# The norms of a fused ten-phase block go to the head of every engine's row, and one MLP leaves another tile of each half to its end

## The chip, the cores and the metric

The kernel runs on one core of a Trainium2 chip. The metric is the device time of one execution in microseconds; the median of several runs is compared. A core has a matrix engine (TensorE, PE in the rows; PEld is its weight load), VectorE (DVE), ScalarE (ACT), GpSimd (POOL) and SyncE (SP, which issues most transfers here). Each of these engines takes its instructions from its own row, one after the other; semaphores make it wait for the others.

## The reference

Two residual blocks run one after the other on x of 256 x 1024 in float32. The first has four sublayers (windowed attention, squared-ReLU MLP, a gated recurrent block, MLP), each modulated by a condition c, the second has six (feed-forward, hybrid mixer, feed-forward, twice). Cut to what matters here:

```
def layer_norm(x, g, b):
    mu = mean(x); var = mean((x - mu)**2)
    return (x - mu) * rsqrt(var + 1e-5) * g + b

for i in range(2):                              # first block
    shift, scale, gate = split(silu(c) @ ada_w[i, 0] + ada_b[i, 0])
    y = mixer(x * (1 + scale) + shift)          # attention (i = 0) or recurrent block (i = 1)
    x = layer_norm(sqrt(2) * x + (1 + gate) * y, ln_g[i, 0], ln_b[i, 0])
    shift, scale, gate = split(silu(c) @ ada_w[i, 1] + ada_b[i, 1])
    y = square(relu((x * (1 + scale) + shift) @ w1[i])) @ w2[i]
    x = layer_norm(sqrt(2) * x + (1 + gate) * y, ln_g[i, 1], ln_b[i, 1])
# the second block has the same norm behind each of its six sublayers, without shift, scale and gate
```

So there are ten norms. Four of them stand behind a modulated sublayer, and the first three also stand in front of one.

## The kernel before

x stays on the chip as two tiles of 128 rows (X[0] and X[1], in the rows X_76 and X_77: the two "halves"). The ten phases run one after the other, in the order attn, mlp0, rnn, mlp1, ffn00, mix0, ffn01, ffn10, mix1, ffn11. Weights stream in from HBM in units of 128 x 2048 (raw, L346). ScalarE rounds each tile of a unit to a part hi (L365; VectorE by a copy at L363 for some), and VectorE subtracts this to get lo (L369). Activations are split likewise (L382 on ScalarE, L384 on VectorE, into tT and hT). Each product is then three matmuls, hi x hi, hi x lo and lo x hi: L393 to L395 and L402 to L404 for the first matrix of a phase (into pu), L429 to L431 for the second one (into four accumulators acc[half, c], c being a half of the 1024 columns).

A phase's second matrix comes in tiles (class Down): 32 in an MLP, 22 in a feed-forward, 8 in the attention, 12 in the recurrent block. The last LAG = 4 tiles of each half are left for the end (`tail`), so that half 0 can be finished while TensorE still has half 1 to do. `finish` (L691) then goes, for each half, through the tail's matmuls, the norm (`ln_stats`, L628) and the turn to the layout of the next phase (`turn`, L653).

The norm's steps for one half, each on 512 columns where nothing else is said: t = acc x g1 (L636, only behind a modulated sublayer), X = sqrt(2) X + t (L638), statistics (L639), then aggregation (L641) and adding epsilon (L642) on one column, the power -1/2 on GpSimd (L643). In front of a modulated phase L650 makes the bias and ScalarE normalises (L652). In the other norms (`ln["direct"]`) VectorE does it in two steps (L646, L648). Then TensorE transposes eight blocks of 128 x 128 (L661), and these are evacuated with shift and scale by VectorE and ScalarE in turn (L668, L670) or by ScalarE alone (L663) into h. TensorE multiplies this h by the first, unsplit weights of the next phase in plain float32 (head_mm, L688; each of these instructions has two records in the profile).

Other work runs alongside the norms on VectorE: the first weight splits of the next phase, in quarters of 256 columns for the first seven tiles (L369), and the sums of the next modulations (aacc, L481 and L483, one step per row of 128 of the ada matrix).

What sets the order: the program is written in one sequence, and a scheduler merges it into one row per engine, by rank of each instruction (its place in the program, with instructions under `tc.high_priority()` ahead of all others) and by its own estimate of when operands are ready. `turn` is under `tc.high_priority()` already. At the six norms ahead of an unmodulated phase TensorE's row is written by hand (`tc.manual_schedule`): tail of half 0, tail of half 1 without its last product, turn of half 0, the last product, matmuls of the next phase, turn of half 1.

Of the kernel before, what the change touches and what calls it, by code (L numbers as in the profile page):

```python
# [25 lines left out]
LAG = 4  # L26
# [24 lines left out]
ADA = {"attn": (0, 0), "mlp0": (0, 1), "rnn": (1, 0), "mlp1": (1, 1)}  # L51
# [3 lines left out]
def nf(ph):  # L55

    return NF.get(ph, 3)
# [47 lines left out]
def items_of(ph):  # L105

    if ph == "attn":
        out = [("k", 0), ("k", 1), ("v", 0), ("v", 1)] + [("q", h) for h in range(4)]
        for h in range(8):
            if h < 4:  # L110
                out.append(("q", h + 4))
            if h >= 2:
                out.append(("o", h - 2))
        return out + [("o", 6), ("o", 7)]
    if ph in ("mlp0", "mlp1"):
        return ff_items(32, ("u",))
    if ph.startswith("ffn"):
        return ff_items(22, ("g", "u"))
    if ph == "rnn":
        x = [("x", t) for t in range(12)]  # L120
        g = [("g", t) for t in range(12)]
        b = [("b", j) for j in range(12)]
        o = [("o", k) for k in range(12)]
        return (x[:5] + b[:3] + g[:1] + x[5:8] + b[3:6] + g[1:3] + x[8:] + b[6:9] + g[3:6] + b[9:] + o[:3] + g[6:9] + o[3:6]
                + g[9:] + o[6:])
    out = [("ka", 0), ("ka", 1), ("k", 0), ("va", 0), ("va", 1), ("va", 2), ("qa", 0)]
    name = {"c": lambda n: MIX_CONVS[n + 1], "q": lambda n: ("qa", n), "g": lambda n: ("ga", n)}
    out += [name[ev](n) for ev, n in mix_seq() if ev in name]
    for j in range(8):
        out += [("ba", j)] if ("ga", j) in out else [("ga", j), ("ba", j)]  # L130
        if j % 4 == 3:
            out += [("z", j // 4, q) for q in range(4)]
    out += [("gb", j) for j in range(4)]
    for j in range(8):
        out.append(("bb", j))
        if j < 4:
            out.append(("gb", j + 4))
        if j >= 2:
            out.append(("o", j - 2))
    return out + [("o", 6), ("o", 7), ("pad", 0)]  # L140
# [147 lines left out]
def fused_kernel(ctx, tc, x, wst, adaw, ada0, rows, rowc, cols, vecs, relb, cst, m1, rope, oh, out, phases=PH_ALL):  # L288
# [14 lines left out]
    def ps_acc(name="pa"):  # L303
        return pacc.tile([128, 512], F32, tag="acc", name=name)
# [101 lines left out]
    def joined(pool, ps, tag):  # L406

        if ps.shape[1] == 256:
            return ps
        t = pool.tile([128, 256], F32, tag=tag, bufs=3, name=tag)  # L410
        S.activation(out=t, in_=ps[:, 256:512], func=AF.Copy)
        V.tensor_tensor(out=t, in0=ps[:, 0:256], in1=t, op=ALU.add)
        return t
# [138 lines left out]
    def ada_tasks(lst, pe=False):  # L552
        seq = [(i, s, p, k) for i, s, p in lst for k in range(8)]
        for n in range(len(seq) + 5):
            def task(n=n):
                if n < len(seq):
                    ada_load(*seq[n])
                if pe:
                    if 0 <= n - 3 < len(seq) and (n - 3) % 2:
                        ada_mm(*seq[n - 4])  # L560
                    if n >= 5 and seq[n - 5][3] == 7:
                        ada_end(*seq[n - 5][:3])
                    return
                if 0 <= n - 3 < len(seq):
                    ada_mac(*seq[n - 3])
                if n >= 5 and seq[n - 5][3] == 7:
                    ada_sum(*seq[n - 5][:3])
            side.append(task)
# [57 lines left out]
            ln["ha"], ln["hb"] = ha, hb  # L626

    def ln_stats(half, acc, last):  # L628
        pool = ln["pool"]
        stt = pool.tile([128, 2, 6], F32, tag="st", bufs=2, name="stt")  # L630
        cs_ = [slice(c * 512, c * 512 + 512) for c in range(2)]
        src = [acc[half, c] for c in range(2)]
        for c, s in enumerate(cs_):
            if ln["g1"] is not None:
                t = pool.tile([128, 512], F32, tag="t1", bufs=2, name="t1")
                V.tensor_tensor(out=t, in0=src[c], in1=ln["g1"][:, s], op=ALU.mult)  # L636
                src[c] = t
            V.scalar_tensor_tensor(out=X[half][:, s], in0=X[half][:, s], scalar=SQ2, in1=src[c], op0=ALU.mult, op1=ALU.add)  # L638
            V.bn_stats(out=stt[:, c, :], in_=X[half][:, s])  # L639
        mv = pool.tile([128, 3], F32, tag="mv", bufs=2, name="mv")  # L640
        V.bn_aggr(out=mv[:, 0:2], in_=stt)  # L641
        V.tensor_scalar(out=mv[:, 1:2], in0=mv[:, 1:2], scalar1=LN_EPS, scalar2=None, op0=ALU.add)  # L642
        G.tensor_tensor(out=mv[:, 2:3], in0=mv[:, 1:2], in1=mhalf[:, 0:1], op=ALU.pow)  # L643
        if last:
            for s in cs_:
                V.scalar_tensor_tensor(out=X[half][:, s], in0=X[half][:, s], scalar=mv[:, 0:1], in1=ln["g"][:, s], op0=ALU.subtract, op1=ALU.mult)  # L646
            for s in cs_:
                ins = V.scalar_tensor_tensor(out=X[half][:, s], in0=X[half][:, s], scalar=mv[:, 2:3], in1=ln["b"][:, s], op0=ALU.mult, op1=ALU.add)  # L648
            return ins
        V.scalar_tensor_tensor(out=mv[:, 1:2], in0=mv[:, 0:1], scalar=-1.0, in1=mv[:, 2:3], op0=ALU.mult, op1=ALU.mult)  # L650
        for s in cs_:
            S.activation(out=X[half][:, s], in_=X[half][:, s], func=AF.Identity, scale=mv[:, 2:3], bias=mv[:, 1:2])  # L652
# [89 lines left out]
    class Down:  # L742


        def __init__(self, n):
            self.n, self.k, self.acc, self.tail = n, 0, {}, {0: [], 1: []}

        def add(self, t, w):
            if not self.acc:
                self.acc = {(h, c): ps_acc("acc") for h in range(2) for c in range(2)}  # L750
            if self.k >= self.n - LAG:
                for half in range(2):
                    self.tail[half].append((t, w))
            else:
                for half in range(2):
                    self.part(half, t, w, self.k == 0)
            self.k += 1
# [114 lines left out]
    def ph_mlp(ph, nxt):  # L872
        pool = state["es"].enter_context(tc.tile_pool(name="ml", bufs=1))
        tT = {}
        dn = Down(32)
        if ph == "mlp0":
            ada_tasks([(0, 1, 2)] + ([(1, 0, p) for p in range(3)] + [(1, 1, 0)] if nxt in ADA else []))
        else:
            ada_tasks([(1, 1, 2)])
            if has_mix:  # L880
                side.insert(0, lambda: bias_load(pool))
                side.append(bias_table)
        for it in items_of(ph):
            if it[0] == "u":
                u = joined(pool, up(ph, *it), "u")
                r = pool.tile([128, 256], F32, tag="r", bufs=3, name="r")
                if it[1] < nf(ph):
                    S.activation(out=r, in_=u, func=AF.Relu)
                    V.tensor_tensor(out=r, in0=r, in1=u, op=ALU.mult)
                else:  # L890
                    V.scalar_tensor_tensor(out=r, in0=u, scalar=0.0, in1=u, op0=ALU.max, op1=ALU.mult)
                t = tT[it[1]] = pool.tile([128, 512], F32R, tag="tT", bufs=LAG + 5, name="tT")
                split(t[:, 0:256], t[:, 256:512], r)
            else:
                if it[1] == 14:
                    xs_todo = x_scale()
                if it[1] in (18, 19) and xs_todo:
                    xs_todo.pop(0)()
                if it[1] == 27:
                    while side:  # L900
                        side.pop(0)()
                    ln_open(ph, nxt)
                w = get(ph, *it)
                dn.add(tT.pop(it[1]), w)
        return dn
# [183 lines left out]
    def bias_load(pool):  # L1089
        rb = pool.tile([32, 16], F32, name="rb")  # L1090
        nc.gpsimd.dma_start(out=rb, in_=relb)
        ohs = pool.tile([32, 128], F32, name="ohs")
        nc.gpsimd.dma_start(out=ohs, in_=oh)
        ext = pool.tile([16, 384], F32, name="ext")
        G.memset(ext, -1e30)
        state["bias"] = rb, ohs, ext
# [650 lines left out]
    for n, ph in enumerate(phases):  # L1747
        nxt = phases[n + 1] if n + 1 < len(phases) else None
# [9 lines left out]
        dn = f(ph, nxt)  # L1758
# [20 lines left out]
```

## Time and profile before

| | us |
|---|---|
| median of 3 runs (lowest to highest) | 2088.3 (2087.17 to 2094.09) |
| the profiled execution | 2087.69 |
| its span, first to last instruction | 2086.0 |
| TensorE busy in it | 2027.6 |
| VectorE busy | 1516.6 |
| ScalarE busy | 1116.8 |

The span is what the profile's lines cover; the profiled execution's own time has 1.7 us more around it. A timeline's row gives the start, the busy time, the engine, the line, the operation, what it writes from what it reads, the shape and the count, and in brackets the idle time of the engine just before, with the instruction that ended it. Consecutive equal instructions share a row.

### The profile page before, as it was taken

What the parts mean: (1) busy time and instruction counts of PE and PEld (TensorE: products, weight loads), DVE (VectorE), ACT (ScalarE), POOL (GpSimd) and SP (SyncE); (2) the same over time, 40 slices, a digit from 0 to 9 for tenths busy, and PEclk for the clock granted to TensorE, in tenths of its full rate; (3) what the DMA queues carried; (4) which work ended last, traced back from release to release, by engine and by line L of the source; (5) the groups of instructions that cost most, each with busy time, mean ns of one, the idle gap of its engine ahead of it and who ended that gap; (6) DMA issues with size and microseconds to landing.
All of it is one profiled execution on the core that took longest, in us unless ns stands there. A gap on an engine that the chain in (4) does not pass through costs nothing. (4 is left out here: it accounts for less than half of the span.)

```text
span 2086.0 us, 34685 instructions
## 1 busy us (share of the span) xinstructions
PE 2027.6 (97%) x13786; PEld 1777.3 (85%) x13786; DVE 1516.6 (73%) x2735; ACT 1116.8 (54%) x1995; POOL 122.3 (6%) x157
## 2 busy tenths in 40 slices
PE   6999999989999999999999999999999999999998
PEld 4788888978888888888989888888889888998886
DVE  2689989987667666789956766676668897667665
ACT  3554446874544555477644455545546774445553
POOL 0000000000000000021011000000001111100000
PEclk9999999999999999999989999999999998999999
DMA  8978884355673655454424465555546434355552
GB/s 335 336 265 329 319 319 183 129 198 187 217 254 131 241 190 194 172 182 140 157 81 180 161 224 195 187 195 189 188 156 215 136 141 157 123 201 182 194 190 81
DMA packets 67698, 409.67 MB, mean 196 GB/s; under 512 B 8240, under 2 KB 8544, under 8 KB 27088
## 3 DMA queue, kind: packets, MB, share of 16 engines
q1 hardware_dynamic: 59952, 383.25, 50.5%
q0 software_dynamic: 7440, 24.03, 3.6%
q8 instruction: 108, 1.77, 0.3%
q14 instruction: 54, 0.44, 0.1%
q10 hardware_dynamic: 144, 0.18, 0.0%
HBM read 406.34 MB, written 4.24 MB: 197 GB/s over the span
## 5 line engine op out<-in xcount | busy, mean ns | idle before, releaser
L369 DVE TENSOR_TENSOR lo<-raw,hi 128x1024 fp32r<-128x1024 f32 (+2 forms) x689 | 729.1, 1069 | 308.8 <-ACT hi L365 299.1
L365 ACT ACTIVATE hi<-raw 128x1024 fp32r<-128x1024 f32 x578 | 605.3, 1053 | 338.2 <-PE pu L402 73.9
L402 PE MATMUL pu<-hT,hi 128*128 128x512 f32 x1760 | 439.2, 392 | 0.0
L402 PEld LDWEIGHTS pu<-hT,hi 128*128 128x128 f32 x1760 | 324.6, 188 | 65.2 <-issue 0.4
L429 PE MATMUL acc<-hi,tT 128*128 128x512 f32 x688 | 271.6, 396 | 3.2 <-ACT tT L382 3.0
L430 PE MATMUL acc<-hi,tT 128*128 128x512 f32 x688 | 271.6, 395 | 0.0
L393 PE MATMUL pu<-hT,hi 128*128 128x256 f32 x928 | 271.4, 292 | 0.0
L431 PE MATMUL acc<-lo,tT 128*128 128x512 f32 x688 | 270.2, 393 | 0.0
L395 PE MATMUL pu<-hT,lo 128*128 128x256 f32 x928 | 265.5, 286 | 2.3 <-DVE lo L369 2.3
L394 PE MATMUL pu<-hT,hi 128*128 128x256 f32 x928 | 265.5, 286 | 0.0
L404 PEld LDWEIGHTS pu<-hT,lo 128*128 128x128 f32 x1760 | 240.2, 191 | 17.1
L404 PE MATMUL pu<-hT,lo 128*128 128x256 f32 x1760 | 245.6, 283 | 0.0
L393 PEld LDWEIGHTS pu<-hT,hi 128*128 128x128 f32 x928 | 178.9, 193 | 12.9 <-issue 10.6
L382 ACT ACTIVATE tT<-r 128x256 fp32r<-128x256 f32 x152 | 63.1, 416 | 235.6 <-DVE r L918 136.9
L394 PEld LDWEIGHTS pu<-hT,hi 128*128 128x128 f32 x928 | 179.1, 193 | 3.0 <-issue 2.6
L395 PEld LDWEIGHTS pu<-hT,lo 128*128 128x128 f32 x928 | 178.9, 193 | 2.7 <-DVE lo L369 2.5
L429 PEld LDWEIGHTS acc<-hi,tT 128*128 128x128 f32 x688 | 130.0, 189 | 29.6 <-ACT tT L382 5.0
L431 PEld LDWEIGHTS acc<-lo,tT 128*128 128x128 f32 x688 | 129.8, 189 | 27.7 <-issue 0.4
L430 PEld LDWEIGHTS acc<-hi,tT 128*128 128x128 f32 x688 | 130.1, 189 | 24.4 <-DVE tT L384 1.6
L688 PE MATMUL hd<-h,raw 128*128 128x128 f32 x960 | 111.4, 276 | 0.0
L688 PEld LDWEIGHTS hd<-h,raw 128*128 128x128 f32 x960 | 109.5, 192 | 1.1
L384 DVE TENSOR_TENSOR tT<-r,tT 128x256 fp32r<-128x256 f32 x152 | 64.6, 426 | 54.8 <-ACT tT L382 54.8
(398 smaller groups left out, 2755.2 us busy)
## 6 DMA issues: line engine op xcount, KB each, us to landing
raw<-wst SPq DMA_DIRECT2D x316, 1024.0 KB, 4.8
aw<-adaw SPq DMA_DIRECT2D x80, 512.0 KB, 6.5
aw<-ada SPq DMA_DIRECT2D x16, 512.0 KB, 7.6
bias<-bias_d POOLq DMA_DIRECT2D x32, 192.0 KB, 2.8
g<-rows POOLq DMA_DIRECT2D x10, 512.0 KB, 4.7
b<-rows POOLq DMA_DIRECT2D x10, 512.0 KB, 5.7
bias_d<-ext_d POOLq DMA_DIRECT2D x1, 2048.0 KB, 20.2
gbc<-g_d POOLq DMA_DIRECT2D x4, 512.0 KB, 4.4
```

Source lines behind the costliest of these rows:

```text
L365: S.activation(out=hi[:, 0:n], in_=r, func=AF.Copy)
L369: V.tensor_tensor(out=lo[:, c:c + m], in0=r[:, c:c + m], in1=hi[:, c:c + m].bitcast(F32), op=ALU.subtract)
L384: (eng or V).tensor_tensor(out=dlo, in0=src, in1=dhi.bitcast(F32), op=ALU.subtract)
L393: T.matmul(ps, lhsT=hi[:, c], rhs=r[:, 0:256], start=kk == 0, stop=False)
L394: T.matmul(ps, lhsT=hi[:, c], rhs=r[:, 256:512], start=False, stop=False)
L395: T.matmul(ps, lhsT=lo[:, c], rhs=r[:, 0:256], start=False, stop=kk == KT - 1)
L402: T.matmul(ps, lhsT=hi[:, kk * 128:kk * 128 + 128], rhs=rhs(kk), start=kk == 0, stop=False)
L404: T.matmul(ps[:, 0:256], lhsT=lo[:, kk * 128:kk * 128 + 128], rhs=rhs(kk)[:, 0:256], start=False, stop=kk == KT - 1)
L429: T.matmul(ps, lhsT=th, rhs=hi, start=first, stop=False)
L430: T.matmul(ps, lhsT=tl, rhs=hi, start=False, stop=False)
L431: T.matmul(ps, lhsT=th, rhs=lo, start=False, stop=last)
L688: T.matmul(ps[:, half * 128:half * 128 + 128], lhsT=w[:, kk * 128:kk * 128 + 128], rhs=state["h32", half][:, kk, :], start=kk == 0, stop=k ...
```

## The change

Two edits. `ln_stats` now calls the old body, renamed `ln_steps`, under `tc.high_priority()`: this holds for all ten norms and for both halves. And `Down` takes the number of tiles to leave for the end; `ph_mlp` gives it five instead of four where the next phase is a modulated one. Of the two MLPs only mlp0 (followed by rnn) is that; mlp1 is followed by ffn00 and keeps four. The buffers stay as they are.

```diff
     def ln_stats(half, acc, last):
+        with tc.high_priority():
+            return ln_steps(half, acc, last)
+
+    def ln_steps(half, acc, last):
+
         pool = ln["pool"]
...
-        def __init__(self, n):
-            self.n, self.k, self.acc, self.tail = n, 0, {}, {0: [], 1: []}
+        def __init__(self, n, tail=LAG):
+            self.n, self.k, self.acc, self.tail, self.last = n, 0, {}, {0: [], 1: []}, tail
...
-            if self.k >= self.n - LAG:
+            if self.k >= self.n - self.last:
...
-        dn = Down(32)
+
+        dn = Down(32, LAG + 1 if nxt in ADA else LAG)
```

The new kernel's lines are five (norm, turn) or six (further down) higher: L636 is L641 there, L638 is L643, L639 is L644, L641 is L646, L642 is L647, L646 is L651, L648 is L653, L650 is L655, L661 is L666, L668 is L673, L688 is L693.

VectorE at the first norm (attention to mlp0), before; the names t_ are the products with g1, the first two of half 76 and then two of half 77:

```order
L639 BN_STATS stt<-X_76 128x6 x2
L636 TENSOR_TENSOR t_1209<-acc,g_1117 128x512
L641 BN_AGGR mv<-stt 128x2
L636 TENSOR_TENSOR t_1213<-acc,g_1117 128x512
L642 TENSOR_SCALAR mv<-mv 128x1
L638 SCALAR_TENSOR_TENSOR X_77<-X_77,t_1209 128x512
L650 SCALAR_TENSOR_TENSOR mv<-mv 128x1
L638 SCALAR_TENSOR_TENSOR X_77<-X_77,t_1213 128x512
L639 BN_STATS stt<-X_77 128x6 x2
```

And in the new kernel, from the same place:

```order
L641 TENSOR_TENSOR t_1209<-acc,g_1117 128x512
L644 BN_STATS stt<-X_76 128x6
L643 SCALAR_TENSOR_TENSOR X_77<-X_77,t_1209 128x512
L641 TENSOR_TENSOR t_1213<-acc,g_1117 128x512
L644 BN_STATS stt<-X_77 128x6
L643 SCALAR_TENSOR_TENSOR X_77<-X_77,t_1213 128x512
L644 BN_STATS stt<-X_76 128x6
L644 BN_STATS stt<-X_77 128x6
L646 BN_AGGR mv<-stt 128x2
L369 TENSOR_TENSOR lo<-raw,hi 128x256
L646 BN_AGGR mv<-stt 128x2
```

Half 76's second statistics step stands behind the last product of half 77 and its statistics behind that; the small steps of half 76 follow after all large steps of both halves.

TensorE behind that, before (pt are the transposes, hd the first products of the next phase):

```order
L431 MATMUL acc<-lo,tT 128x512
L661 MATMUL pt<-cs,X_76 128x128 x8
L688 MATMUL hd<-h_1224,raw 128x128 x19
L661 MATMUL pt<-cs,X_77 128x128 x4
L688 MATMUL hd<-h_1224,raw 128x128
L661 MATMUL pt<-cs,X_77 128x128 x4
L688 MATMUL hd<-h_1224,raw 128x128 x12
L688 MATMUL hd<-h_1306,raw 128x128 x32
```

And now:

```order
L431 MATMUL acc<-lo,tT 128x512
L666 MATMUL pt<-cs,X_76 128x128 x5
L666 MATMUL pt<-cs,X_77 128x128 x5
L666 MATMUL pt<-cs,X_76 128x128
L666 MATMUL pt<-cs,X_77 128x128
L666 MATMUL pt<-cs,X_76 128x128
L666 MATMUL pt<-cs,X_77 128x128
L666 MATMUL pt<-cs,X_76 128x128
L666 MATMUL pt<-cs,X_77 128x128
L693 MATMUL hd<-h_1224,raw 128x128 x32
L693 MATMUL hd<-h_1306,raw 128x128 x32
```

All transposes of both halves stand ahead of the first matmul of the next phase; before, the second half's came between.

VectorE at the second norm (mlp0 to rnn), before, from half 76's second statistics step on (t_2983 and t_2987 are half 77's products, aacc a step of a modulation):

```order
L639 BN_STATS stt<-X_76 128x6
L636 TENSOR_TENSOR t_2983<-acc,g_2851 128x512
L641 BN_AGGR mv<-stt 128x2
L483 SCALAR_TENSOR_TENSOR aacc<-aw,csil,aacc 128x1024
L642 TENSOR_SCALAR mv<-mv 128x1
L638 SCALAR_TENSOR_TENSOR X_77<-X_77,t_2983 128x512
L650 SCALAR_TENSOR_TENSOR mv<-mv 128x1
L636 TENSOR_TENSOR t_2987<-acc,g_2851 128x512
L639 BN_STATS stt<-X_77 128x6
L638 SCALAR_TENSOR_TENSOR X_77<-X_77,t_2987 128x512
```

And now, from the first product of half 77 on:

```order
L641 TENSOR_TENSOR t_2983<-acc,g_2851 128x512
L644 BN_STATS stt<-X_76 128x6
L643 SCALAR_TENSOR_TENSOR X_77<-X_77,t_2983 128x512
L646 BN_AGGR mv<-stt 128x2
L363 CAST hi<-raw 128x1024
L644 BN_STATS stt<-X_77 128x6
L647 TENSOR_SCALAR mv<-mv 128x1
L369 TENSOR_TENSOR lo<-raw,hi 128x256
L641 TENSOR_TENSOR t_2987<-acc,g_2851 128x512
L655 SCALAR_TENSOR_TENSOR mv<-mv 128x1
L369 TENSOR_TENSOR lo<-raw,hi 128x256
L643 SCALAR_TENSOR_TENSOR X_77<-X_77,t_2987 128x512
```

Half 77's first product and sum, a weight copy and its second product now stand ahead of half 76's last small step; the modulation's step is gone from between them, further ahead.

VectorE at the norm ahead of the first mixer (X_76 and X_77 are the halves of x, g and b the norm's own rows), before:

```order
L641 BN_AGGR mv<-stt 128x2
L642 TENSOR_SCALAR mv<-mv 128x1
L646 SCALAR_TENSOR_TENSOR X_76<-X_76,mv,g 128x512 x2
L648 SCALAR_TENSOR_TENSOR X_76<-X_76,mv,b 128x512 x2
L638 SCALAR_TENSOR_TENSOR X_77<-X_77,acc 128x512
L369 TENSOR_TENSOR lo<-raw,hi 128x256
L639 BN_STATS stt<-X_77 128x6
```

And now:

```order
L646 BN_AGGR mv<-stt 128x2
L647 TENSOR_SCALAR mv<-mv 128x1
L651 SCALAR_TENSOR_TENSOR X_76<-X_76,mv,g 128x512 x2
L643 SCALAR_TENSOR_TENSOR X_77<-X_77,acc 128x512
L653 SCALAR_TENSOR_TENSOR X_76<-X_76,mv,b 128x512
L644 BN_STATS stt<-X_77 128x6
L653 SCALAR_TENSOR_TENSOR X_76<-X_76,mv,b 128x512
```

A sum of half 77 and its statistics stand between the last steps of half 76. The other five norms of that kind have the same two steps there.

ScalarE in the recurrent phase, at the third group of gates (a and r are gate steps on 256 columns, tT the split of a product for the second matrix, gl that product, hi the weight splits), before:

```order
L1009 ACTIVATE a<-r,sp 128x256 x2
L1010 ACTIVATE r<-r,sp 128x256 x2
L1009 ACTIVATE a<-r,sp 128x256 x2
L1010 ACTIVATE r<-r,sp 128x256 x2
L382 ACTIVATE tT<-gl 128x256
L365 ACTIVATE hi<-raw 128x1024
L1015 ACT_TABLE_LOAD
L1015 ACTIVATE r<-r 128x1536
```

And now:

```order
L1015 ACTIVATE a<-r,sp 128x256 x2
L1016 ACTIVATE r<-r,sp 128x256 x2
L1015 ACTIVATE a<-r,sp 128x256 x2
L1016 ACTIVATE r<-r,sp 128x256 x2
L365 ACTIVATE hi<-raw 128x1024 x2
L1021 ACT_TABLE_LOAD
L1021 ACTIVATE r<-r 128x1536
```

The split into tT is gone from behind the gate steps: it stands some forty rows further up, with the two others of its group, and two weight splits stand in its place.

## Rows read from the trace of the kernel before

**Rows 1.** The page: busy time of each engine; TensorE's granted clock in 40 slices

```profile
PE 2027.6 (97%) x13786; PEld 1777.3 (85%) x13786; DVE 1516.6 (73%) x2735; ACT 1116.8 (54%) x1995; POOL 122.3 (6%) x157
...
PEclk9999999999999999999989999999999998999999
```

**Rows 2.** The timeline of VectorE, then ScalarE, at the first norm

```profile
129.24 0.69 DVE L636 TENSOR_TENSOR t<-acc,g 128x512 f32<-128x512 f32 x1 [0.20 <-PE acc L431]
129.84 0.14 DVE L642 TENSOR_SCALAR mv<-mv 128x1 f32<-128x1 f32 x1
...
131.08 0.16 DVE L650 SCALAR_TENSOR_TENSOR mv<-mv 128x1 f32<-128x1 f32 x1 [0.49 <-POOL mv L643]
...
131.27 1.52 ACT L652 ACTIVATE X<-X,mv 128x512 f32<-128x512 f32 x2 [2.41 <-DVE mv L650]
```

**Rows 3.** The timeline of TensorE at the first norm

```profile
132.14 1.36 PE L661 MATMUL pt<-cs,X 128*128 128x128 f32 x8 [2.94 <-ACT X L652]
133.34 4.51 PE L688 MATMUL hd<-h,raw 128*128 128x128 f32 x38
...
148.53 0.48 PE L429 MATMUL acc<-hi,tT 128*128 128x512 f32 x1
```

**Rows 4.** Four stretches: length, busy time (instructions) of each engine, granted clock, DMA share, GB/s

```profile
132.10:133.30 1.20, 1.11 (x8) 0.84 (x8) 1.20 (x3) 1.15 (x2) 0.00 (x0) 1.00 0.00 0
431.60:434.40 2.80, 0.00 (x1) 0.00 (x0) 2.15 (x4) 2.80 (x8) 0.00 (x0) 1.00 0.00 0
435.50:436.20 0.70, 0.70 (x4) 0.51 (x3) 0.70 (x2) 0.70 (x1) 0.00 (x0) 0.50 0.00 0
445.00:448.40 3.40, 3.40 (x18) 3.40 (x18) 3.40 (x4) 1.46 (x3) 1.28 (x2) 0.51 0.26 28
```

**Rows 5.** The timeline of VectorE, then TensorE, at the second norm

```profile
319.97 1.23 DVE L483 SCALAR_TENSOR_TENSOR aacc<-aw,csil,aacc 128x1024 f32<-128x1024 f32 x1
321.12 0.15 DVE L642 TENSOR_SCALAR mv<-mv 128x1 f32<-128x1 f32 x1
...
322.36 0.16 DVE L650 SCALAR_TENSOR_TENSOR mv<-mv 128x1 f32<-128x1 f32 x1 [0.49 <-POOL mv L643]
...
321.04 0.40 PE L429 MATMUL acc<-hi,tT 128*128 128x512 f32 x1
...
321.51 0.39 PE L431 MATMUL acc<-lo,tT 128*128 128x512 f32 x1
323.42 1.36 PE L661 MATMUL pt<-cs,X 128*128 128x128 f32 x8 [1.52 <-ACT X L652]
324.62 4.73 PE L688 MATMUL hd<-h,raw 128*128 128x128 f32 x40
```

**Rows 6.** The timeline of VectorE, then TensorE, at the third norm

```profile
485.52 0.16 DVE L650 SCALAR_TENSOR_TENSOR mv<-mv 128x1 f32<-128x1 f32 x1 [0.49 <-POOL mv L643]
...
486.58 0.66 PE L661 MATMUL pt<-cs,X 128*128 128x128 f32 x4 [1.27 <-ACT X L652]
...
492.91 0.66 PE L661 MATMUL pt<-cs,X 128*128 128x128 f32 x4 [0.39 <-ACT X L652]
```

**Rows 7.** The timeline of VectorE, then TensorE, at the norm before the mixer

```profile
859.18 1.41 DVE L648 SCALAR_TENSOR_TENSOR X<-X,mv,b 128x512 f32<-128x512 f32 x2
...
859.98 1.32 PE L661 MATMUL pt<-cs,X 128*128 128x128 f32 x8 [0.18 <-DVE X L648]
...
866.79 0.66 PE L661 MATMUL pt<-cs,X 128*128 128x128 f32 x4 [0.56 <-DVE X L648]
```

**Rows 8.** The timeline of ScalarE, VectorE and TensorE in the recurrent phase

```profile
434.01 0.40 ACT L382 ACTIVATE tT<-gl 128x256 fp32r<-128x256 f32 x1
...
439.94 3.59 DVE L1029 TENSOR_TENSOR_SCAN r<-a,i 128x256 f32<-128x256 f32 x6
...
434.46 1.93 PE L429 MATMUL acc<-hi,tT 128*128 128x512 f32 x4 [2.86 <-ACT tT L382]
...
444.70 0.43 PE L395 MATMUL pu<-hT,lo 128*128 128x256 f32 x1 [2.28 <-DVE lo L369]
```

## The prediction

> **What bounds the kernel now.** I read the busy lines of the page first. TensorE is busy for 2027.6 of 2086.0 us, 97%, and its clock line shows nines in all but two slices [rows 1]. So almost everything that the other engines do is hidden, and a change of their order can cost or gain only where TensorE stands still. I then read TensorE's own idle times. The longer ones stand at two kinds of place: where one phase ends and the next begins (the norm has to be done before its output can be transposed and multiplied), and inside the recurrent phase. Both are the places that this change touches. The gaps at the ten norms before: 2.94 us at the first [rows 3], 1.52 at the second [rows 5], 1.27 and 0.39 at the third [rows 6], then 0.18 and 0.56 at a typical one of the later six [rows 7]. The reader should see from this that there is little to win: all these gaps together are some 10 us of 2086.
>
> **The change, part by part.** It adds no arithmetic and no transfer: the same instructions run, in another order, and a norm's steps issue no DMA. The first edit puts the norms' steps first on every engine, but gives the steps of both halves the same rank. What each step takes is known from the rows; what is new is who stands ahead of whom, and VectorE and ScalarE work through their rows strictly in that order. So I replay each norm with the durations of before and the rows of the new order.
>
> **First norm (attention to MLP).** Before, VectorE had finished half 76 apart from its small steps when it came to the last product of half 77 at 129.24, which waited 0.20 for TensorE's sums; L642 of half 76 ran at 129.84 and L650 at 131.08 [rows 2]. In the new order half 76's second statistics step stands behind that product, and four steps of 512 columns are ahead of the aggregation. Rows of that size follow each other every 0.60 us (129.24 to 129.84). So aggregation comes at 129.24 + 5 x 0.60 = 132.24, and with a piece of a weight split and the other half's aggregation between, L642 at about 132.85: 3.0 later. The same chain behind it (1.24 to L650, 0.19 to ScalarE, 0.87 to TensorE, from 129.84, 131.08, 131.27, 132.14) puts the first transpose at 135.15 instead of 132.14, an idle time of about 6 us instead of 2.94. Then ScalarE takes the halves in turn, 0.76 each (two take 1.52 [rows 2]), and TensorE's row is all sixteen transposes before any matmul of the next phase; the last of them waits for the fourth normalising step, which ends near 137.7, and six short ones of 0.15 follow. The next phase's matmuls start at 138.65. Before they started at 133.34 with eight transposes (1.06 us) still to come between them, and ended at 148.53 [rows 3]; like for like that is 138.65 - 134.40 = 4.3 later. Two ada steps of the kind that takes 1.23 [rows 5] now stand on VectorE between the evacuations that these matmuls read, for which I add 0.6. Sum 4.9; the bounds are 3.0 (only the delay of the chain) and 5.5.
>
> **The clock there.** The granted clock stayed at 1.00 behind the 2.94 us of before [rows 4]. [...]
>
> **Second norm (MLP to recurrent), with the second edit.** Five tiles of each half instead of four are left for the end, so half 76's sums are ready one tile earlier: a tile is six matmuls of a half, which follow each other every 0.233 us (321.04 to 321.51 [rows 5]), 1.4 us in all. The work is the same, so half 77 ends as before, at 321.90, and its first sums, 15 matmuls earlier, at 318.4. The chain of half 76 before ran L641, an ada step of 1.23, L642 at 321.12, L650 at 322.36 [rows 5]. In the new order that ada step and a second are further ahead, but the first product and sum of half 77 (0.60 each) and a weight copy of 0.69 are put ahead of half 76's small steps, and that product waits for those first sums. From there come product, statistics, sum, aggregation, copy and statistics, and then L642: 318.4 + 0.6 + 0.6 + 0.6 + 0.2 + 0.7 + 0.6 = 321.7, with some 0.5 for waits between dependent steps 322.2, 1.1 late. The last product of half 77 is also ahead of L650. So the transposes start at 324.5 instead of 323.42. Those of half 77 then stand after 22 matmul records instead of 40 (324.62 [rows 5]; each instruction has two), which is not enough to cover its chain: another 1.1. Term 2.2, bounds -1.5 (the idle time of before is gone) and 4.
>
> **Third norm (recurrent to MLP).** A product, a sum and a statistics step of half 77 come ahead of L642 and L650. L650 moves from 485.52 [rows 6] by about 1.6, and half 77's transposes stand after fewer matmuls. Term 1.8, bounds 0 and 3.
>
> **The six norms in front of the second block's phases.** TensorE's own order is written by hand there and hardly changes. On VectorE the two L648 steps of half 76 ran together (1.41 from 859.18), and the transposes followed with a wait of 0.18 [rows 7]. Now a sum of half 77 stands before the first of the pair and its statistics before the second, 0.60 each. Half 76's second four transposes wait 0.6 to 1.2 longer, and the last matmuls of half 77 stand behind them on TensorE. Half 77's chain starts from these, so nothing is given back. 0.6 each, 3.6 in all, bounds 0 and 6. At the last norm nothing follows on TensorE: 0. Elsewhere (the mixer's scores, the MLP) the order shifts by a step here and there under a TensorE that doesn't wait: 0, bounds -2 and 2.
>
> **The recurrent phase.** This phase has no edit of its own, but its rows are ordered anew. ScalarE's split of a product (434.01) stood behind six pairs of gate steps, and TensorE waited 2.86 for it; later six scans, 3.59 in all, stood ahead of a weight split, and TensorE waited 2.28 [rows 8]. In the new order that split stands forty rows up, ahead of these gates, and two weight splits follow them; the scans remain ahead of the weight split. Of the most that this could give (2.86 + 2.28 and 1.5 + 1.7 for the two stretches at half clock, 8.3 together) I take 3.0, about the first wait; the work that is behind the gates must still wait for them. Bounds -8.3 and 1.
>
> **Sum.** 4.9 + 1.5 + 2.2 + 1.8 + 3.6 - 3.0 = 11.0 us. The profiled execution took 2087.69 us in all, with a span of 2086.0; the median of the three runs is 2088.3. Against the profiled one the sum gives 2098.7, against the median 2099.3. I forecast **2099.0**.
>
> **The rivals.**
> *The recurrent phase gives everything back.* If its two waits and both half-clock stretches go, 8.3 us come back, and with the norms at the lower part of their bounds (3.0 at the first, 1.1, 1.2 and six times 0.2, sum 6.5) the time is 1.8 less than before: 2086.5, not slower. For it: both waits were for steps that stood in the queue, not for a transfer. Against it: ScalarE is busy without a break through 431.6 to 434.4, 2.80 of 2.80, while TensorE stands still [rows 4], so moving one step up moves others down. It decides if the first norm costs less than 4 us. Chance 0.17.
> *The priority does what its name says.* The chain of a half is shorter than what stands around it: without the weight pieces and the ada step the second norm would be ready 3.2 us sooner and, with the extra tile, TensorE would not wait at all. Then the gaps of the second and third norm (1.52 and 1.27), and the recurrent phase's 8.3, are saved, with the first norm as it was: 2088.3 - 11.1 = 2077. Against it: the rows show half 77's waiting steps between half 76's, in all three. Chance 0.08.
> *The clock stays up behind the first norm.* Then 2097.5, slower all the same. For it: the 2.94 us of before left it up. Chance 0.15.
> *The edit at the MLP does nothing.* One tile more or less at the end moves no work if the norm sets the time there; this is part of the forecast, at 1.4 us at the most.
>
> **How the numbers follow.** The forecast has 0.60. The range takes in the first rival's upper side, down to 2088 (the lower bounds of single terms rarely meet), and 2106 above (5.5 + 1.7 + 4 + 3 + 4, with nothing from the recurrent phase, is 18). A difference of 0.3%, 6.3 us, is what a measurement of this kernel can tell from none: 2082.0 and 2094.6 are its borders. Faster: the second rival and a little of the first, 0.10. Within: most of the first and the lowest end of the forecast, 0.20. Slower: the rest, 0.70.
>
> **What would show it.** In the new profile: TensorE's gap ahead of the first norm's transposes near 6 us, and a granted clock near 0.5 behind it; the sixteen transposes in one run before the next phase's matmuls; gaps above 2 us at the second and third norm; at the later six a gap of half a microsecond in or behind half 76's transposes; in the recurrent phase the 2.86 us gap gone or smaller. It is wrong if the first norm's gap is under 4 us, or if TensorE's idle time in the recurrent phase falls by more than 6.

## The result

The changed kernel takes 2101.0 us (median of 4 runs, 2096.97 to 2102.25) against 2087.7 for the kernel before in the same call (4 runs, 2086.34 to 2094.09): a ratio of 1.0061, 95% interval 1.0044 to 1.0078. It is slower by some 13 us, and clear of noise. The forecast was 2099.0, with a range of 2088 to 2106, slower at 0.70.

The page of the changed kernel, its busy line and its clock line:

```profile
span 2098.4 us, 34689 instructions
...
PE 2035.2 (97%) x13786; PEld 1783.7 (85%) x13786; DVE 1519.2 (72%) x2735; ACT 1116.0 (53%) x1995; POOL 127.1 (6%) x157
...
PEclk9999999999999999999989999999999999999999
```

The busy lines say little, as before [rows 1]: TensorE is busy 97% of both. Its 7.6 us more of busy time are the same number of matmuls, some of them at a lower clock (its mean was 0.984 in this profile, 0.990 in that of before). What changed is read stage by stage. I took two points of each norm from TensorE's timeline, the end of the last product ahead of it and the end of the first matmuls of the next phase, and subtracted those of the profile before. "Norm" is the time from the one to the other, "phase" from there to the next norm; the last column is the position lost so far.

| stretch | change in us | lost so far |
|---|---|---|
| up to the first norm | +0.6 | 0.6 |
| first norm (attention to MLP) | +4.8 | 5.4 |
| MLP | -0.3 | 5.1 |
| second norm | +0.5 | 5.6 |
| recurrent phase | -1.5 | 4.1 |
| third norm | +4.4 | 8.5 |
| MLP | 0.0 | 8.5 |
| fourth norm (MLP to feed-forward) | +2.6 | 11.2 |
| fifth to ninth norm | +0.3, +0.3, +0.3, +0.6, +0.5 | |
| phases between these, and the end | +0.7, -1.4 (the mixers), -0.2 (the end), else 0 | 12.4 |

Three of the norms, the first, the third and the fourth, carry 11.8 of the 12.4 us.

This is one profile against one, and the clock has a share in it. The runs of one kernel differ in their mean granted clock, and the time goes with it: the kernel before took 2082.7 us in a run at 0.992 and 2093.2 to 2095.8 in its four at 0.983 or 0.984 (of its 60 runs beside the experiments). Three of the changed kernel's four runs were at 0.984 and took 2100.1 to 2102.3. So at an equal clock the change costs some 6 to 7 us, and about half of the 13 us goes with a lower clock.

**First norm.** VectorE, then TensorE, of the changed kernel:

```profile
129.85 0.69 DVE L641 TENSOR_TENSOR t<-acc,g 128x512 f32<-128x512 f32 x1 [0.21 <-PE acc L431]
130.46 0.68 DVE L644 BATCH_NORM_STATS2 stt<-X 128x6 f32<-128x512 f32 x1
131.06 0.68 DVE L643 SCALAR_TENSOR_TENSOR X<-X,t 128x512 f32<-128x512 f32 x1
131.65 1.28 DVE L644 BATCH_NORM_STATS2 stt<-X 128x6 f32<-128x512 f32 x2
...
133.37 0.10 DVE L647 TENSOR_SCALAR mv<-mv 128x1 f32<-128x1 f32 x1
...
134.29 0.16 DVE L655 SCALAR_TENSOR_TENSOR mv<-mv 128x1 f32<-128x1 f32 x1 [0.43 <-POOL mv L648]
...
135.35 1.12 PE L666 MATMUL pt<-cs,X 128*128 128x128 f32 x4 [5.53 <-ACT X L657]
136.76 2.82 PE L666 MATMUL pt<-cs,X 128*128 128x128 f32 x12 [0.30 <-ACT X L657]
139.38 14.85 PE L693 MATMUL hd<-h,raw 128*128 128x128 f32 x128
153.98 0.47 PE L429 MATMUL acc<-hi,tT 128*128 128x512 f32 x1
```

The wait of 0.21 for half 77's last sums is where it was [rows 2], but behind that product four more large steps, three of them half 77's, now come ahead of half 76's small ones. TensorE waits 5.53 us instead of 2.94 [rows 3] and then does sixteen transposes ahead of any matmul of the next phase. The granted clock of these stretches (the column after the five engines):

```profile
129.85:135.30 5.45, 0.00 (x0) 0.00 (x0) 4.98 (x16) 0.82 (x2) 1.16 (x2) 0.82 0.01 2
135.30:136.70 1.40, 1.12 (x4) 0.72 (x4) 1.40 (x3) 1.40 (x3) 0.00 (x0) 0.50 0.00 0
136.70:139.40 2.70, 2.64 (x13) 2.52 (x14) 2.70 (x5) 1.86 (x5) 0.00 (x0) 0.50 0.70 206
142.00:145.00 3.00, 3.00 (x29) 3.00 (x28) 3.00 (x4) 3.00 (x4) 1.25 (x2) 1.00 0.83 295
```

The clock did fall in the wait (1.00 up to 132.00, 0.50 from 133.50) and stayed at 0.50 until the transposes were done; the first matmuls behind it take 14.85 us for 128 records, no more than the 14.89 of before (4.51 + 0.39 + 9.99). The price of the clock lies on the transposes. Here is ScalarE's last normalising step in the changed kernel, and TensorE in the kernel before:

```profile
136.95 0.80 ACT L657 ACTIVATE X<-X,mv 128x512 f32<-128x512 f32 x1
```

```profile
137.69 0.60 PE L661 MATMUL pt<-cs,X 128*128 128x128 f32 x4
138.13 0.39 PE L688 MATMUL hd<-h,raw 128*128 128x128 f32 x2
...
138.79 9.99 PE L688 MATMUL hd<-h,raw 128*128 128x128 f32 x88
```

The twelve transposes behind the wait of 0.30 follow each other every 0.22 us without a break (136.76 to 139.38), twice the 0.11 of before (four from 137.69 to 138.13). At 0.11 each they would have waited for ScalarE's last step, which ends at 137.75, and the seven from there on would have been done at about 138.6. By this estimate the clock cost some 0.8 us on the transposes, and some 0.4 on the matmuls behind them (2.6 us at 0.85 from 139.40 to 142.00): 1.2 of the 4.8.

**Third norm.** SyncE's issue, ScalarE, VectorE and TensorE of the changed kernel:

```profile
476.75 1.21 DVE L369 TENSOR_TENSOR lo<-raw,hi 128x1024 fp32r<-128x1024 f32 x1
...
477.99 0.33 SPq L346 DMA_DIRECT2D raw<-wst  x1
...
482.84 2.01 ACT L365 ACTIVATE hi<-raw 128x1024 fp32r<-128x1024 f32 x2 [3.33 <-DMA raw<-wst]
...
483.93 0.42 DVE L369 TENSOR_TENSOR lo<-raw,hi 128x256 fp32r<-128x256 f32 x1 [3.83 <-ACT hi L365]
484.28 0.68 DVE L641 TENSOR_TENSOR t<-acc,g 128x512 f32<-128x512 f32 x1
...
492.73 0.15 DVE L655 SCALAR_TENSOR_TENSOR mv<-mv 128x1 f32<-128x1 f32 x1
...
493.79 1.97 PE L666 MATMUL pt<-cs,X 128*128 128x128 f32 x8 [4.35 <-ACT X L657]
495.55 1.98 PE L693 MATMUL hd<-h,raw 128*128 128x128 f32 x8
```

And the rows of the kernel before that answer to the first five:

```profile
471.18 1.22 DVE L369 TENSOR_TENSOR lo<-raw,hi 128x1024 fp32r<-128x1024 f32 x1
...
472.42 0.33 SPq L346 DMA_DIRECT2D raw<-wst  x1
...
477.18 2.01 ACT L365 ACTIVATE hi<-raw 128x1024 fp32r<-128x1024 f32 x2 [3.25 <-DMA raw<-wst]
...
478.28 0.43 DVE L369 TENSOR_TENSOR lo<-raw,hi 128x256 fp32r<-128x256 f32 x1 [3.88 <-ACT hi L365]
478.62 0.68 DVE L636 TENSOR_TENSOR t<-acc,g 128x512 f32<-128x512 f32 x1
```

In both kernels the norm's first step stands on VectorE behind a piece of the next phase's weight split, and this waits for a transfer that was issued only when the last split of the recurrent phase (476.75, 471.18) had freed a buffer, 0.03 and 0.02 us behind the end of that split. So the chain's start moved by 5.66 us, as the whole phase's start had (5.6), while TensorE's last product moved by 4.1 only: TensorE's 1.5 us from the recurrent phase are given back here. From its first step to L655 the chain takes 8.45 us instead of 6.90, 1.55 more for half 77's steps in it. Together L655 stands 3.1 us later behind the last product; the remaining 1.3 of the 4.4 are the lower clock (0.50 and 0.57 in the next two rows, 1.00 only from 499), less the wait of 0.39 for half 77 [rows 6], which is gone.

```profile
493.80:496.00 2.20, 2.20 (x10) 2.11 (x11) 1.32 (x5) 1.51 (x3) 0.70 (x2) 0.50 0.95 396
496.00:499.00 3.00, 3.00 (x18) 3.00 (x17) 0.50 (x2) 2.03 (x5) 0.00 (x0) 0.57 0.01 3
499.00:502.00 3.00, 3.00 (x29) 3.00 (x28) 2.47 (x8) 3.00 (x6) 0.00 (x0) 1.00 0.01 3
```

**Fourth norm.** TensorE's two waits for half 76's last steps in its timeline, and the stretch behind them, with its clock:

```profile
680.79 0.66 PE L666 MATMUL pt<-cs,X 128*128 128x128 f32 x4 [1.12 <-DVE X L653]
682.05 0.66 PE L666 MATMUL pt<-cs,X 128*128 128x128 f32 x4 [0.60 <-DVE X L653]
```

```profile
683.00:686.50 3.50, 3.50 (x17) 3.31 (x16) 2.94 (x7) 1.39 (x2) 0.09 (x1) 0.53 0.56 171
```

At this norm half 77's product with g1 stands between half 76's steps as well, three in all. Before, there was no wait here, and one of 0.56 for half 77 later, which is gone now. 1.72 - 0.56 and some 1.5 for the 3.5 us at a clock of 0.53 are the 2.6. At the five later norms the two waits are 0.52 and 0.60 or one of 0.44 to 0.60.

**Second norm.** Its wait is 1.78 instead of 1.52 [rows 5], in spite of the mixing: the fifth tile gave half 76's chain an earlier start (x5 below has the same norm without it).

```profile
328.81 1.36 PE L666 MATMUL pt<-cs,X 128*128 128x128 f32 x8 [1.78 <-ACT X L657]
...
332.90 0.66 PE L666 MATMUL pt<-cs,X 128*128 128x128 f32 x4 [0.16 <-ACT X L657]
```

### The profile page after: what moved, and what is told of

Same layout as the page of the kernel before. It is cut to its first block, busy times and chain, and to the rows that moved or that the text cites. A ratio compares the mean times of both kernels' runs of the same rounds, so it can differ in the third digit from the quotient of the medians.

```text
span 2098.4 us, 34689 instructions
## 1 busy us (share of the span) xinstructions
PE 2035.2 (97%) x13786; PEld 1783.7 (85%) x13786; DVE 1519.2 (72%) x2735; ACT 1116.0 (53%) x1995; POOL 127.1 (6%) x157
## 4 chain that ended last, share of the span: by engine, by line
PE 82%; DVE 9%; DMA 3%; ACT 3%; issue 2%; POOL 0%; DVEq 0%; SPq 0%; ACTq 0%; POOLq 0%
PE pu L402 19%; PE pu L404 10%; PE acc L430 7%; PE acc L429 7%; PE acc L431 7%; PE hd L693 5%; PE pu L393 4%; PE pu L394 4%; PE pu L395 4%; DVE lo L369 2%; DMA raw<-wst 2%; PE py L393 2%; PE py L394 2%; PE py L395 2%; PE gp L1001 1%
## 5 line engine op out<-in xcount | busy, mean ns | idle before, releaser
L693 PE MATMUL hd<-h,raw 128*128 128x128 f32 x960 | 114.0, 279 | 0.0
L693 PEld LDWEIGHTS hd<-h,raw 128*128 128x128 f32 x960 | 112.5, 196 | 1.4 <-ACT h L668 0.6
```

The lines of the kernel that those rows point to most:

```text
L693: T.matmul(ps[:, half * 128:half * 128 + 128], lhsT=w[:, kk * 128:kk * 128 + 128], rhs=state["h32", half][:, kk, :], start=kk == 0, stop=k ...
```

## The experiments

The theory: the change costs because half 77's steps, which wait for their own sums, get into half 76's chain. Rival 1: the fifth tile and the new order of the recurrent phase cost. Rival 2: raising the norms above the weight splits and ada sums costs as such, since these come too late. Times are medians beside the runs of the kernel before in the same call (2088.9 for the first four experiments, 2088.3 for the other four).

**Only the norms ahead of a modulated phase (x1_modulated_only).**

```diff
-        with tc.high_priority():
-            return ln_steps(half, acc, last)
+        if not ln["direct"]:
+            with tc.high_priority():
+                return ln_steps(half, acc, last)
+        return ln_steps(half, acc, last)
...
-        dn = Down(32, LAG + 1 if nxt in ADA else LAG)
+        dn = Down(32, LAG)
```

> The norm's steps of both halves are first only at the three norms ahead of a modulated phase; the others are as before, and the MLP leaves four tiles. Theory (the halves' steps get between each other on VectorE): the first norm costs 4.8 as in the changed kernel; at the second, with four tiles, half 77's last product (sums ready at 321.90) stands ahead of half 76's L642, so the transposes come 2.6 later than 323.42; the third costs 2 to 4. In all about +10, 2098 us, against 2087.7 before. Rival 1 (the fifth tile and the recurrent phase's new order cost the time): under +5, below 2093. Rival 2 (weight splits pushed back by any priority cost it): as the theory, but with waits of TensorE for lo or hi behind the norms.

Measured: 2096.5 us, ratio 1.0027 (1.0011 to 1.0044), slower. In its profile the first norm costs 4.5, the second 5.4, the third 2.4, and the fourth nothing. TensorE at the second norm:

```profile
331.00 1.54 PE L668 MATMUL pt<-cs,X 128*128 128x128 f32 x6 [4.17 <-ACT X L659]
332.74 2.39 PE L668 MATMUL pt<-cs,X 128*128 128x128 f32 x10 [0.20 <-ACT X L659]
334.93 15.63 PE L695 MATMUL hd<-h,raw 128*128 128x128 f32 x128
```

The wait is 4.17 instead of 1.52: 2.65 more, where 2.6 was expected for half 77's last product ahead of half 76's L642. The other 2.7 of this norm's 5.4 lie behind the wait, where the granted clock was 0.50 up to 334.90 and 0.60 from there to 338.00 (1.00 over the whole norm before). With four tiles this norm shows what the first one does, all sixteen transposes ahead of the matmuls. No wait for lo or hi stands behind these norms.

**Only the other norms (x2_direct_only).** The same edit with `if ln["direct"]`.

> The norm's steps of both halves are first only at the six norms ahead of an unmodulated phase and the last one; four tiles. Theory: the two gaps inside half 76's transposes (1.12 and 0.60 at the fourth norm, 0.5 and 0.6 at the others) come back here without the first three norms, 2.6 at the fourth and 0.3 to 0.6 at the others, in all +4.7, 2092.4 us. Rival 1: no change, 2088. Rival 2: +4.7 as well, but behind waits for weight splits.

Measured: 2091.8 us, ratio 1.0009 (0.9990 to 1.0027): by the runs alone it can't be told from no change. By the profile it can: the fourth norm takes 1.1 more and the five later ones 0.5, 0.3, 0.3, 0.6 and 0.5, 3.3 in all. TensorE's timeline at the fourth norm, and the stretch with its clock (the column after the five engines):

```profile
673.74 0.66 PE L668 MATMUL pt<-cs,X 128*128 128x128 f32 x4 [1.11 <-DVE X L655]
674.99 0.66 PE L668 MATMUL pt<-cs,X 128*128 128x128 f32 x4 [0.60 <-DVE X L655]
```

```profile
672.50:676.50 4.00, 2.29 (x15) 1.79 (x15) 3.89 (x9) 1.38 (x3) 0.00 (x0) 1.00 0.00 0
```

The waits are those of the changed kernel, 1.11 and 0.60, but the clock stayed at 1.00 here. So the fourth norm's 2.6 is 1.1 of order and 1.5 of clock, and the expectation, which took the 2.6 for order, was high by that. Two of the kernels below repeat it with the same two waits: x5 lost 2.6 here, with 0.55 from 683.00 to 686.50, and x6 1.2, with 1.00 from 680.80 to 688.00.

**Only the fifth tile (x3_five_tiles_only).** The changed kernel without `tc.high_priority()`.

> Only the fifth tile left to the end at the MLP ahead of the recurrent phase; no priority. Theory: the second norm within 1 us of before (the product of half 77 is still ahead of half 76's statistics, but L650 isn't behind the last product), the recurrent phase about 1.5 shorter, and this given back at the third norm, whose chain begins behind a weight split that waits for a transfer: 2087 to 2089 us, no change. Rival 1: +7 or more, 2095.

Measured: 2090.6 us, ratio 1.0010 (0.9996 to 1.0023), no change; rival 1 falls. The second norm takes 0.6 less than before, the recurrent phase 1.5 less, the third norm 2.7 more, and VectorE's first row there is as it was foreseen:

```profile
472.79 1.21 DVE L369 TENSOR_TENSOR lo<-raw,hi 128x1024 fp32r<-128x1024 f32 x1
...
479.92 0.43 DVE L369 TENSOR_TENSOR lo<-raw,hi 128x256 fp32r<-128x256 f32 x1 [3.79 <-ACT hi L365]
480.26 0.68 DVE L640 TENSOR_TENSOR t<-acc,g 128x512 f32<-128x512 f32 x1
```

The chain starts 1.64 later than before (478.62), TensorE's last product comes at the same time (485.30), and TensorE waits 2.92 instead of 1.27. That the recurrent phase's gain is lost to this transfer needs no priority. The wait is 1.65 of the 2.7; the rest lies behind it, at a granted clock of 0.54 from 488.20 to 491.80.

**All norms first, the halves apart (x4_halves_apart).** VectorE's steps of half 77 are queued behind the last one of half 76.

```diff
         with tc.high_priority():
-            return ln_steps(half, acc, last)
+            if half == 0:
+                return ln_steps(half, acc, last)
+            with tc.issue_after(ln["done"].ins):
+                return ln_steps(half, acc, last)
...
+            ln["done"] = ins
...
-        V.scalar_tensor_tensor(out=mv[:, 1:2], in0=mv[:, 0:1], scalar=-1.0, ...)
+        ln["done"] = V.scalar_tensor_tensor(out=mv[:, 1:2], in0=mv[:, 0:1], scalar=-1.0, ...)
...
-        dn = Down(32, LAG + 1 if nxt in ADA else LAG)
+        dn = Down(32, LAG)
```

> All norms' steps first on every engine, as in the changed kernel, but VectorE's steps of half 77 are queued behind half 76's last VectorE step (L650, or L648 where there is no modulation); four tiles. Theory: the cost is in the mixing of the halves, so it goes: first norm -0.5 against before, second +1 (three ada steps stand ahead of L650), third +0.5, the later ones 0: 2088.5 us. Rival 2 (any priority of the norms over the splits and ada steps costs): like the changed kernel, 2098 to 2101.

Measured: 2089.2 us, ratio 0.9995 (0.9980 to 1.0011): the loss is gone with the priority still there. This decides for the theory against rival 2. Nor is it the clock alone: the profiled run of this kernel was at a mean granted clock of 0.984, like that of the changed one, and took 2091.3 us against 2100.1. At the first norm TensorE's wait is even shorter than before:

```profile
131.69 1.36 PE L670 MATMUL pt<-cs,X 128*128 128x128 f32 x8 [1.81 <-ACT X L661]
132.89 5.46 PE L697 MATMUL hd<-h,raw 128*128 128x128 f32 x32
```

The norm as a whole takes 0.5 more all the same, where 0.5 less was expected: the 32 records behind the transposes take 5.46, at a granted clock of 0.55 from 133.00 to 136.80. The second norm costs 3.0 more, where 1 was expected. Its wait is 3.08 instead of 1.52, since three ada steps of 1.3 now stand among half 76's small steps; the other 1.5 lie behind it, at a granted clock of 0.53 from 327.90 to 331.30. The third is 1.0 shorter.

**Only the first edit (x5_priority_four_tiles).** The changed kernel with `Down(32, LAG)`.

> Only the first edit: the norm's steps of both halves first at all ten norms, four tiles at the MLP. Theory: the sum of the two parts measured alone (profiles: +8.7 with the modulated norms, +3.3 with the others): +12 us, about 2100, the same as the changed kernel; the fifth tile then changes nothing in the whole, but moves time: without it the second norm costs 5 more (8.0 us from the last down product to the end of the next phase's first matmuls more than before: 5.4), the recurrent phase and the third norm 4 to 5 less. Rival 1 (the fifth tile costs): 2093 or less.

Measured: 2100.4 us, ratio 1.0053 (1.0034 to 1.0073), as the changed kernel; the fifth tile changes nothing in the whole. It moves time as expected in kind. Against the kernel before, the second norm costs 4.2 without it (0.5 with it), the recurrent phase gives 0.9 (1.5) and the third norm costs 0.5 (4.4). The third norm's wait is 1.70 here. The chain's first step came 7.1 us later than before (485.69) and TensorE's last product 8.4, so that TensorE's own lateness covered most of what the mixing added to the chain (8.67 from its first step to L655, 6.90 before).

**Only half 77 first (x6_half_77_only).**

```diff
-        with tc.high_priority():
-            return ln_steps(half, acc, last)
+        if half == 1:
+            with tc.high_priority():
+                return ln_steps(half, acc, last)
+        return ln_steps(half, acc, last)
```

> Priority for the second half's (77's) norm steps alone, five tiles. The other way round, priority for the first half alone, leaves every row of TensorE, VectorE and ScalarE as without any priority, so it needs no run. Theory: the second half's steps are what moves, so this gives all of the changed kernel's loss: +11 to +13, 2099 to 2102 us. Rival 2 (any priority over the weight splits costs, in proportion to the steps raised): about half, 2094.

Measured: 2099.2 us, ratio 1.0047 (1.0030 to 1.0064): all of the loss within the noise, with a wait of 5.53 at the first norm and 4.42 at the third. Half 76's steps stood first anyway; the priority lifted only those of half 77.

**The weight splits behind the norm (x7_splits_behind_norm, and with five tiles x8_splits_behind_five_tiles).** An attempt to use what the third norm shows, on the kernel before, without any priority for the norms' steps:

```diff
-        V.scalar_tensor_tensor(out=mv[:, 1:2], in0=mv[:, 0:1], scalar=-1.0, ...)
+        ln["done"] = V.scalar_tensor_tensor(out=mv[:, 1:2], in0=mv[:, 0:1], scalar=-1.0, ...)
...
-                head_mm(0, keys, hps, 8 * len(keys) - (1 if ln["g1"] is not None else 5), lambda: turn_(1))
                 with tc.issue_after(ins.ins):
+                    head_mm(0, keys, hps, 8 * len(keys) - (1 if ln["g1"] is not None else 5), lambda: turn_(1))
                     turn_split(0, hT)
...
-                head_mm(half, keys, hps)
+                with tc.issue_after(ln["done"].ins):
+                    head_mm(half, keys, hps)
```

> The kernel before, without any priority for the norms and with four tiles, but the next phase's first weight splits (lo on VectorE) and its hT split are queued behind the second half's last VectorE step of the norm (L650, L648). Theory: the norm's chain at the third norm began behind a split that waited for a transfer (478.28, idle 3.88), so its gap of 1.27 goes, and those of 0.56 and 0.17 at the later norms; the second is unchanged within 1: -2 to -3, 2086 us. Rival (the splits are needed soon, so TensorE waits for them behind the norm's matmuls): the gaps come back there as waits for lo, +2 or more.

Measured: 2088.2 us, ratio 0.9996 (0.9986 to 1.0007), no change. The runs alone don't exclude the 2 us that were expected; the expectation falls by the profile. The six later norms did gain, 3.2 us together: their waits of 0.18 to 0.56 are gone. But at the second norm the ada sums took the place that the splits had left (a wait of 2.91, 2.8 lost, half of it behind the wait, where the granted clock was 0.51 from 328.50 to 332.00), and at the third the wait stayed 1.26 though no split stood ahead of the chain. VectorE, with GpSimd's one step:

```profile
481.46 0.69 DVE L636 TENSOR_TENSOR t<-acc,g 128x512 f32<-128x512 f32 x1 [1.04 <-PE acc L431]
...
484.26 0.69 DVE L636 TENSOR_TENSOR t<-acc,g 128x512 f32<-128x512 f32 x1 [0.65 <-PE acc L431]
...
487.70 0.59 POOL L643 TENSOR_TENSOR mv<-mv,mhalf 128x1 f32<-128x1 f32 x1 [7.43 <-DVE mv L642]
488.32 0.16 DVE L650 SCALAR_TENSOR_TENSOR mv<-mv 128x1 f32<-128x1 f32 x1 [1.49 <-POOL mv L643]
```

VectorE now waits for TensorE's sums, as it should, and then 1.49 for GpSimd, more than the 0.49 of before [rows 6]. GpSimd's step took no longer than before (0.59, 0.63 there) but began 0.87 behind the end of L642, where that was 0.16 before. What held it there stays open; in x8 it began after 0.15 again.

> As the kernel with the splits behind the norm, with five tiles left at the MLP. Theory: the five tiles alone made the recurrent phase 1.5 shorter and this was given back at the third norm, where the chain waited for a transfer; with the splits out of the chain it stays: 1 to 1.5 less than with four tiles, 2085 us. Rival (the recurrent phase's gain is lost anyway, since weights come when they come): the same as with four tiles.

Measured: 2086.2 us (12 runs, 2083.82 to 2088.02), ratio 0.9987 (0.9977 to 0.9997): 2 us less than the kernel before, and some 15 less than the changed one. It is the fastest kernel of the study, by little. The number came as expected; that it came by the expected mechanism is not shown. The recurrent phase is 1.4 us longer here than before, not shorter, but its clock was another one. The whole phase in this kernel and in the one before (the clock is the column after the five engines):

```profile
341.05:487.57 146.52, 139.10 (x969) 126.46 (x968) 127.00 (x203) 111.48 (x192) 9.85 (x7) 0.94 0.47 170
```

```profile
340.23:485.31 145.08, 136.68 (x975) 123.90 (x974) 127.94 (x205) 110.40 (x190) 4.00 (x7) 0.98 0.44 162
```

TensorE stood still for 7.4 us in it, 8.4 before. Against x7 the profile gains at the second norm, 0.4 instead of 2.8 (half of that was x7's clock of 0.51), and at the third, with a wait of 0.58.

## Why the prediction was right, step by step

**First norm.** 4.9 of order and 1.5 of clock were forecast, 6.4; 4.8 was measured. L647 stands 3.5 behind the last product's start on VectorE's row (129.85 to 133.37), forecast 3.6; the transposes begin 5.53 behind TensorE's last product, forecast about 6, since the way from L647 to L655 took 0.92 instead of the 1.24 of before. The clock fell, as forecast. No run shows the 1.5 that the sum has for it; the changed kernel showed 0.50 from 133.50 to 139.40 and 0.85 from there to 142.00, and by the estimate above this cost 1.2 of the 4.8. That leaves 3.6 for the order: this is the mis-sized term, by 1.3. The transposes began 0.4 earlier than forecast; the 0.6 for two ada steps between the evacuations doesn't show (14.85 us for the 128 records, 14.89 before); and the short transposes were taken at 0.15 each, where the rows have 0.11. A slip goes the other way: the eight transposes of before, taken as 1.06 us, took two times 0.44.

**Second norm.** 2.2 was forecast, 0.5 measured. The order was read rightly, but I added 0.5 for waits between steps that weren't there, and 1.1 for half 77's chain, whose transposes waited only 0.16. The value lies inside the bounds of -1.5 to 4; the gap of 1.78 is below the 2 us that the prediction named as a sign. Without the fifth tile the term would have been 4.2 to 5.4, clock included (x5, x1), so the second edit did shield this norm, which the forecast valued at 1.4 us at the most.

**Third norm.** 1.8 was forecast, 4.4 measured, above the upper bound of 3. The step that failed: I took the chain's start as fixed to TensorE's last product. It was fixed to a transfer. 1.55 of the 4.4 is the mixing of halves, close to the forecast 1.6; 1.5 is the late start, and 1.3 the clock (0.50 and 0.57) less the gone wait, for both of which the forecast had nothing.

**The six later norms.** 3.6 was forecast, 4.7 measured: 2.6 at the fourth and 2.1 at the others. The order alone gives 3.3 (x2). The two 0.6 steps in half 76's last pair are in the rows as drawn; that the fourth norm has three steps there was in the order and not in my sum, but it costs little (1.1), and the clock (0.53 for 3.5 us) the rest.

**The recurrent phase.** -3.0 was forecast, -1.5 measured. The wait of 2.86 [rows 8] shrank to 0.71 and 0.45, as foreseen, but the next one grew from 2.28 to 3.21 and one of 1.79 at the first gates took the place of two of 0.81 and 1.09. How much of the 1.5 is the new order's doing stays open: x2, whose instructions stand in the order of before up to the fourth norm, came out 1.0 shorter in this phase as well. And the 1.5 came to nothing at the third norm. Taken together, recurrent phase and third norm were forecast at -1.2 and came at +2.9.

**The sum.** 11.0 was forecast, 12.4 measured by the profile and 13.3 by the medians. It was right in size partly because its errors had both signs: -1.6 and -1.7 at the first two norms, +2.6, +1.1 and +1.5 behind them. And about half of it goes with the clock, for which the forecast had 1.5 us, at one norm: the way and the main mechanism were forecast, the size is in part luck. Of the rivals, the recurrent phase giving everything back is refuted (-1.5 of -8.3), the priority as a gain as well (x5), and the clock didn't stay up at the first norm (0.50). Mixing of the halves as the cause is shown by x4 and x6.

## What to carry to other kernels

A priority moves only what stood behind something: read from the order which steps it lifts. Here the first half's steps were first already, and raising both halves alike lifted the second half's steps, which wait for later sums, into the chain that the matrix engine waits for. When work is staggered in two halves to hide a chain, give the halves different ranks, and look at what the first step of the chain stands behind; if that is a transfer, time won ahead of it can come back as a wait, as in x3.

## What the runs showed of the hardware

At the first norm the kernel before and x2 and x3 have the same instructions in the same order and the same wait of 2.94 us on TensorE. In the profile of before the granted clock stayed at 1.00 behind the wait [rows 4], and on to 137.00; in that of x2 it was 0.52 there:

```profile
133.60:136.90 3.30, 3.27 (x16) 3.12 (x17) 2.90 (x10) 2.34 (x5) 0.00 (x0) 0.52 0.00 0
```

That norm took 1.3 us longer in x2 and 1.2 in x3 than in the profile of before. The fourth norm shows the same: waits of 1.12 and 0.60 with a clock of 0.53 in the changed kernel, 1.11 and 0.60 with 1.00 in x2. Behind one and the same wait the clock went either way. So single profiles of this kernel differ by 1.2 to 1.5 us at a norm without any difference in its code there. Terms of that size are told from one profile only where the clock beside them is read too. Over all runs the clock is lower with the change: its mean is 0.9842 to 0.9856 in the changed kernel, x1, x5 and x6, where the halves mix ahead of a modulated phase, and 0.9860 to 0.9880 in the kernel before and the other five.
